# One of seven weight products: its low part from a VectorE subtraction instead of an accumulating GpSimd transfer

## The chip, the cores and the metric

The kernel runs on one core of a Trainium2 chip. The metric is device time of one launch in microseconds (us); the median of three runs is shown for the kernel before. The profiled execution is a fourth run of the same program, and all durations below come from it.

## The reference, cut to what matters

A two-layer block over 256 latent tokens (x) and 256 context tokens (c), 1024 features each. Every layer is half-step SwiGLU FFN, a mixer with three branches, and a second FFN:

```
def swiglu(u, w1, w3, w2):
    return (jax.nn.silu(u @ w1) * (u @ w3)) @ w2

def ffn_sublayer(h, mod, w1, w3, w2, g, b):
    u = h * (1 + mod[1]) + mod[0]
    return layer_norm(ALPHA * h + 0.5 * mod[2] * swiglu(u, w1, w3, w2), g, b)
```

All matrices are float32, w1 and w3 are 1024 x 2816, w2 is 2816 x 1024. Only the products with w1 and w3 of two of the four FFNs are touched by the change.

## The kernel before, in words

Each float32 operand is split into a high part (fp32r, rounded) and a low part (what is left), and a product is three matmuls: high x high, high x low, low x high. The high part is a ScalarE (ACT) copy, the low part a VectorE (DVE) subtraction; `split_into` (L228) does both. Weights stream from HBM through five `raw` buffers, loaded by SyncE's queue (SP), into five high and five low buffers (the names end in `hi` and `lo`).

In two FFNs (the second of layer 0 and the first of layer 1) the 18 hidden tiles 4 to 21 don't multiply w1 and w3 by x and c one by one. `wquads` (L193) forms sums of quarters of both weight tiles, `Blocks` sums of the operands, and seven block products of 12 matmuls each (128x128 by 128x256) replace eight. So there are 36 such tiles. Of each, `wquads` makes four weight pairs: **wa** (the w1 tile as it is), **wd** (the second half of the w3 tile), **wc** (sums written over the w1 buffer), **wb** (sums written over the w3 buffer, `r3`). The sums are the four DVE additions L214 to L217. For wa, wd and wc, `split_into` is used. For wb the low part is made in another way: ACT writes the high part (L222), ACT copies it negated into the low buffer (L223), and a DMA from GpSimd's queue adds `r3` to it in place (L224).

The order on the matmul engine (PE) is written out in `more` (L614), with `blocks_end` keeping the blocks in line. For one tile: two blocks on wa; one on wd of the tile before (`x_blocks`); one on wc (`third_block`, operand tH); one on wc of the tile before (`ctx_blocks`, operand op); two on wb (`last_blocks`, L590, operand tH). In a block, the third matmul (L265) is the first that reads a low part. After each block DVE and ACT take its result from PSUM: ACT L575 copies the first wa block into cc, L594 the last wb block into cv; DVE L583, L595, L601, L606, L608 combine 128x256 tiles; ACT L229 and DVE L230 split the finished 128x512 tile into gh and gl. Between them DVE runs jobs of the conditioning vector in the background (L289, L291, `acc`, 128x512 each, on `araw` loads through the same five raw buffers).

Instructions of one engine run in the order that the scheduler of the framework fixed when the program was built; `high_priority` lets the weight work of a tile go ahead of the tile's own products. Buffers are taken in that order too: as the trace shows, the high part of wb waits until PE has left the high part of wa of the same tile.

Of the kernel before, what the change touches and what calls it, by code (L numbers as in the profile page):

```python
# [8 lines left out]
F32 = mybir.dt.float32  # L9
F32R = mybir.dt.float32r  # L10
AF = mybir.ActivationFunctionType
ALU = mybir.AluOpType
# [39 lines left out]
def hybrid_kernel(tc, x, ctx, pos, cc, wada, pcol, w1, w3, w2a, w2b, wst, wv, wg, wbr, wout, dfc, dft, idn, lnrow, out):  # L52
    nc = tc.nc
# [11 lines left out]
    def nm(s):  # L65
        cnt[0] += 1
        return f"{s}_{cnt[0]}"
# [32 lines left out]
    act = nc.scalar.activation  # L100
# [75 lines left out]
    def tick():  # L176
        debt[0] += rate[0]
        n = int(debt[0])
        debt[0] -= n
        bg(n)  # L180
# [12 lines left out]
    def wquads(src1, src3):  # L193


        tick()
        H = slice(0, 512), slice(512, 1024)
        with tc.high_priority(offset=PRE):
            raw = []
            for src in (src1, src3):  # L200
                t = wp.tile([P, 1024], F32, tag="raw", bufs=NR, name=nm("raw"))
                nc.sync.dma_start(out=t, in_=src)
                raw.append(t)
            r1, r3 = raw

            def halves(name, w=1024):
                return [wp.tile([P, 1024], F32R, tag=t, bufs=NW, name=nm(name + t))[:, :w] for t in ("hi", "lo")]

            a = halves("wa")
            split_into(a[0], a[1], r1)  # L210
            d = halves("wd", 512)
            split_into(d[0], d[1], r3[:, H[1]])
            add = dict(op=ALU.add)
            V.tensor_tensor(r3[:, H[1]], r3[:, H[0]], r3[:, H[1]], **add)  # L214
            V.tensor_tensor(r3[:, H[0]], r3[:, H[0]], r1[:, H[0]], **add)
            V.tensor_tensor(r1[:, H[0]], r3[:, H[1]], r1[:, H[0]], **add)
            V.tensor_tensor(r1[:, H[1]], r1[:, H[0]], r1[:, H[1]], **add)  # L217
            c = halves("wc")
            split_into(c[0], c[1], r1)

            b = halves("wb")
            act(b[0], r3, AF.Copy)  # L222
            act(b[1], b[0].bitcast(F32), AF.Copy, scale=-1.0)  # L223
            nc.gpsimd.dma_start(out=b[1].bitcast(F32), in_=r3, accum_op=ALU.add)  # L224

        return (a, 0), (a, 512), (d, 0), (b, 512), (c, 0), (b, 0), (c, 512)

    def split_into(h, l, src):  # L228
        first = act(h, src, AF.Copy)  # L229
        return first, V.tensor_tensor(l, src, h.bitcast(F32), op=ALU.subtract)  # L230
# [304 lines left out]
    def ffn(l, i, X, ys, T, nxt):  # L535
# [32 lines left out]
        def start_blocks(ft):  # L568

            f = dict(ft=ft, W=wquads(w1[l, i, ft], w3[l, i, ft]))  # L570
            f["r1"] = bank(mmp, "q1")[:, XR]
            f["c"], f["v"] = aslot("cc"), aslot("cv", 256)
            Q[:] = X.operands()
            block(f["r1"], f["W"][0], Q[0], True)
            act(f["c"][:, XR], f["r1"], AF.Copy)  # L575
            return f
# [539 lines left out]
    for part in range(4):  # L1116
# [4 lines left out]
        for kt in range(0, KT, 2):  # L1121
            raw = wp.tile([P, 1024], F32, tag="raw", bufs=NR, name=nm("araw"))
            for k in range(2):
                nc.sync.dma_start(out=raw[:, 512 * k:512 * k + 512].rearrange("p (v c) -> p v c", v=2),
                                  in_=wada[0, (kt + k) * P:(kt + k + 1) * P, 0:2 * D]
# [189 lines left out]
```

## Time and profile before

| | us |
|---|---|
| median of 3 runs (lowest, highest) | 2718.05 (2713.5, 2718.81) |
| profiled execution | 2721.58 |
| its span | 2719.8 |
| PE busy | 2538.8 |
| DVE busy | 1966.5 |
| ACT busy | 1109.8 |
| GpSimd busy | 80.5 |

The span is the time from the first to the last instruction of the profiled execution; around it lie 1.8 us. Busy times of engines overlap, so they don't add up. Matmuls are pipelined: at full clock a row of 0.28 us starts about 0.11 us after the row ahead of it. PEclk in a windows view is the clock that was granted to PE, as a share of 2.4 GHz.

The block products are two parts of the program, from 1224 to 1577 us and from 1674 to 2025 us. Each has three runs of tiles (3, 8 and 7), with products of w2 between them.

### The profile page before, as it was taken

The numbers are of one execution on the slowest core, as the hardware profiler recorded it, in microseconds if no ns is written. First come the engines' busy times: TensorE is split into PE (matmuls) and PEld (weight loads), VectorE is DVE, ScalarE is ACT, GpSimd is POOL, SyncE is SP. The second block draws the span as 40 slices with busy tenths as digits, with TensorE's granted clock in tenths as the row PEclk, the third lists the DMA queues.
The fourth block names the chain that finished last, engine by engine and source line by source line (L and its number), as shares of the span: only waits on it lengthen the run. The fifth ranks groups of instructions, "written<-read, shape, count | busy, mean of one in ns | idle before, by whom it ended". The sixth has DMA issues, their size and how long they took to land. (4 is left out here: it accounts for less than half of the span.)

```text
span 2719.8 us, 40624 instructions
## 1 busy us (share of the span) xinstructions
PE 2538.8 (93%) x15842; PEld 2231.9 (82%) x15842; DVE 1966.5 (72%) x3611; ACT 1109.8 (41%) x1834; POOL 80.5 (3%) x162
## 2 busy tenths in 40 slices
PE   8999999999999999998879799878889999999998
PEld 4777779788778888897767788777779888999998
DVE  5888887888777755587666568656556988987655
ACT  4222235333332324353442446343445334455543
POOL 0000000010100000000000000000000000000000
PEclk9999999999999999998889899988899999999999
DMA  9666663222133233326454444546353333556563
GB/s 287 197 207 191 190 199 108 90 67 89 59 102 96 67 128 97 120 86 170 111 130 133 115 132 133 146 132 178 106 142 99 106 116 119 176 166 210 159 197 125
DMA packets 135744, 372.99 MB, mean 137 GB/s; under 512 B 13313, under 2 KB 28929, under 8 KB 135553
## 3 DMA queue, kind: packets, MB, share of 16 engines
q1 hardware_dynamic: 130368, 351.53, 41.4%
q0 software_dynamic: 5184, 18.88, 3.7%
q8 instruction: 124, 2.03, 0.3%
q14 instruction: 68, 0.55, 0.1%
HBM read 344.11 MB, written 7.34 MB: 129 GB/s over the span
## 5 line engine op out<-in xcount | busy, mean ns | idle before, releaser
L189 ACT ACTIVATE whi<-raw 128x1024 fp32r<-128x1024 f32 (+1 forms) x426 | 444.1, 1044 | 872.6 <-issue 170.1
L190 DVE TENSOR_TENSOR wlo<-raw,whi 128x1024 fp32r<-128x1024 f32 (+1 forms) x426 | 511.5, 1202 | 278.7 <-ACT whi L189 275.6
L673 DVE SCALAR_TENSOR_TENSOR cy<-cz,dww,cy 128x482 f32<-128x482 f32 (+29 forms) x480 | 288.9, 602 | 17.4 <-ACT cy L765 10.5
L291 DVE SCALAR_TENSOR_TENSOR acc<-araw,sc,acc 128x512 f32<-128x512 f32 x392 | 275.1, 746 | 18.2 <-DMA araw<-in_wada_dram 17.3
L265 PE MATMUL q<-tH,wblo 128*128 128x256 f32 x288 | 109.5, 380 | 113.9 <-DMA wblo<-raw 113.9
L265 PEld LDWEIGHTS q<-tH,wblo 128*128 128x128 f32 x288 | 79.0, 274 | 122.5 <-DMA wblo<-raw 122.5
L242 PE MATMUL ffps<-op,whi 128*128 128x256 f32 x608 | 165.3, 281 | 3.9 <-ACT op L229 3.9
L243 PE MATMUL ffps<-op,whi 128*128 128x256 f32 x608 | 168.1, 280 | 0.0
L244 PE MATMUL ffps<-op,wlo 128*128 128x256 f32 x608 | 167.5, 279 | 0.0
L242 PE MATMUL ffps<-opH,whi 128*128 128x512 f32 x352 | 141.0, 403 | 0.7 <-ACT opH L229 0.7
L243 PE MATMUL ffps<-opL,whi 128*128 128x512 f32 x352 | 140.7, 400 | 0.0
L244 PE MATMUL ffps<-opH,wlo 128*128 128x512 f32 x352 | 140.1, 400 | 0.4 <-DVE wlo L190 0.4
L242 PE MATMUL w2ps<-gh,whi 128*128 128x512 f32 x336 | 134.2, 399 | 0.0
L244 PE MATMUL w2ps<-gh,wlo 128*128 128x512 f32 x336 | 133.5, 397 | 0.0
L243 PE MATMUL w2ps<-gl,whi 128*128 128x512 f32 x336 | 133.1, 396 | 0.0
L242 PE MATMUL mg<-opH,whi 128*128 128x512 f32 (+1 forms) x384 | 129.7, 338 | 0.0
L244 PE MATMUL mg<-opH,wlo 128*128 128x512 f32 (+1 forms) x384 | 129.5, 337 | 0.0
L243 PE MATMUL mg<-opL,whi 128*128 128x512 f32 (+1 forms) x384 | 129.4, 337 | 0.0
L242 PEld LDWEIGHTS ffps<-op,whi 128*128 128x128 f32 x608 | 113.0, 190 | 4.8 <-ACT op L229 4.3
L243 PEld LDWEIGHTS ffps<-op,whi 128*128 128x128 f32 x608 | 115.1, 190 | 0.2
L244 PEld LDWEIGHTS ffps<-op,wlo 128*128 128x128 f32 x608 | 114.8, 189 | 0.0
L263 PE MATMUL q<-tH,wbhi 128*128 128x256 f32 x288 | 102.7, 357 | 0.0
(390 smaller groups left out, 7358.0 us busy)
## 6 DMA issues: line engine op xcount, KB each, us to landing
raw<-in_w_dram SPq DMA_DIRECT2D x176, 512.0 KB, 4.1
raw<-in_wst_dram SPq DMA_DIRECT2D x144, 512.0 KB, 3.5
araw<-in_wada_dram SPq DMA_DIRECT2D x128, 512.0 KB, 4.2
raw<-in_w2b_dram SPq DMA_DIRECT2D x64, 512.0 KB, 4.2
raw<-in_wbr_dram SPq DMA_DIRECT2D x48, 512.0 KB, 3.5
wblo<-raw POOLq DMA_DIRECT2D x36, 512.0 KB, 5.3
raw<-in_w2a_dram SPq DMA_DIRECT2D x32, 384.0 KB, 3.2
araw<-in_wada_dram SPq DMA_DIRECT2D x32, 256.0 KB, 5.7
```

Of the source, the lines that this page charges most:

```text
L189: act(hi, raw, AF.Copy)
L190: V.tensor_tensor(lo, raw, hi.bitcast(F32), op=ALU.subtract)
L242: PE.matmul(ps, wh, xh, start=first and i == 0, stop=False)
L243: PE.matmul(ps, wh, xl, start=False, stop=False)
L244: PE.matmul(ps, wl, xh, start=False, stop=last and i == n - 1)
L263: PE.matmul(ps, wh, xh, start=first and k == 0, stop=False, **how)
L265: end = PE.matmul(ps, wl, xh, start=False, stop=k == 3, **how)
L291: V.scalar_tensor_tensor(accs[s], w, c, accs[s], op0=ALU.mult, op1=ALU.add)
L673: V.scalar_tensor_tensor(dv[:, :, a:b], sv[:, :, a + o:b + o], wcols[:, j:j + 1], dv[:, :, a:b], op0=ALU.mult, op1=ALU.add)
```

## The change

The low part of wb is made as the other three are, by `split_into`: one ACT copy for the high part and one DVE subtraction (128x1024) for the low part. The negated ACT copy and the accumulating transfer go.

```
             c = halves("wc")
             split_into(c[0], c[1], r1)
-
             b = halves("wb")
-            act(b[0], r3, AF.Copy)
-            act(b[1], b[0].bitcast(F32), AF.Copy, scale=-1.0)
-            nc.gpsimd.dma_start(out=b[1].bitcast(F32), in_=r3, accum_op=ALU.add)
+            split_into(b[0], b[1], r3)
```

Lines after L223 have a number lower by 3 in the changed kernel: L230 is L227 there, L606 is L603, L595 is L592.

On DVE, in the third run of tiles of the second part, before (wclo, walo, wdlo are low parts; cc and cv are the tile's 128x256 results; the additions of the next tile's weights stand as `raw`):

```order
L217 TENSOR_TENSOR raw_16875<-raw_16875 128x512
L595 TENSOR_TENSOR cv_16769<-q_2575_16843,cv_16769 128x256
L291 SCALAR_TENSOR_TENSOR acc_16870<-araw_17135,sc,acc_16870 128x512 x2
L230 TENSOR_TENSOR wclo_16892<-raw_16875,wchi_16891 128x1024
L583 TENSOR_TENSOR cc_16901<-q_2591_16916,cc_16901 128x256
L601 SCALAR_TENSOR_TENSOR cc_16768<-q_2569_16767,cc_16768 128x256
L230 TENSOR_TENSOR walo_17012<-raw_17007,wahi_17011 128x1024
L606 TENSOR_TENSOR cc_16768<-q_2575_16843,cc_16768 128x256
L230 TENSOR_TENSOR wdlo_17016<-raw_17009,wdhi_17015 128x512
```

The same place on DVE now:

```order
L592 TENSOR_TENSOR cv_16737<-q_2575_16811,cv_16737 128x256
L217 TENSOR_TENSOR raw_16843<-raw_16843 128x512
L288 SCALAR_TENSOR_TENSOR acc_16838<-araw_17101,sc,acc_16838 128x512
L580 TENSOR_TENSOR cc_16868<-q_2591_16883,cc_16868 128x256
L288 SCALAR_TENSOR_TENSOR acc_16838<-araw_17101,sc,acc_16838 128x512
L227 TENSOR_TENSOR wclo_16860<-raw_16843,wchi_16859 128x1024
L227 TENSOR_TENSOR wblo_16864<-raw_16845,wbhi_16863 128x1024
L227 TENSOR_TENSOR walo_16979<-raw_16974,wahi_16978 128x1024
L598 SCALAR_TENSOR_TENSOR cc_16736<-q_2569_16735,cc_16736 128x256
L603 TENSOR_TENSOR cc_16736<-q_2575_16811,cc_16736 128x256
L227 TENSOR_TENSOR wdlo_16983<-raw_16976,wdhi_16982 128x512
```

The subtraction for wblo stands between those for wclo and walo, the step on cv has moved ahead of L217, and the step on cc (L583, now L580) ahead of wclo.

On ACT at the same tile, before:

```order
L594 ACTIVATE cv_16769<-q_2569_16767 128x256
L229 ACTIVATE wchi_16891<-raw_16875 128x1024
L575 ACTIVATE cc_16901<-q_2588_16900 128x256
L222 ACTIVATE wbhi_16895<-raw_16877 128x1024
L223 ACTIVATE wblo_16896<-wbhi_16895 128x1024
L229 ACTIVATE wahi_17011<-raw_17007 128x1024
```

And now:

```order
L591 ACTIVATE cv_16737<-q_2569_16735 128x256
L572 ACTIVATE cc_16868<-q_2588_16867 128x256
L226 ACTIVATE wchi_16859<-raw_16843 128x1024
L226 ACTIVATE wbhi_16863<-raw_16845 128x1024
L581 ACTIVATE cc_16868<-cc_16868 128x256
L226 ACTIVATE wahi_16978<-raw_16974 128x1024
```

The negated copy is gone, and wchi now comes after the copy of the first wa block (L575, now L572). On GpSimd the 36 transfers are gone and nothing else moved; on SP the loads keep their order; on PE the block products keep theirs within a run of tiles.

## Rows read from the trace of the kernel before

**Rows 1.** The page: busy time, share of the span and instructions of each engine.
```profile
PE 2538.8 (93%) x15842; PEld 2231.9 (82%) x15842; DVE 1966.5 (72%) x3611; ACT 1109.8 (41%) x1834; POOL 80.5 (3%) x162
```

**Rows 2.** Waits of the whole span: engine, line, releaser, us in total, times, longest.
```profile
PE q L265 <- DMA wblo<-raw: 113.9, 36, 5.8
```

**Rows 3.** The tile wblo: count, duration ns min/median/max, first and last start; landing times.
```profile
L223 ACT ACTIVATE wblo<-wbhi x36: 1042/1046/1062, 1228.0 to 2015.0; 128x1024 fp32r<-128x1024 f32 x36
DMA to landing us min/median/max: 4.5/5.3/8.3
```

**Rows 4.** Windows: each run's first L575 to its last; one of six, and sum.
```profile
core 0: us, PE busy (x) PEld busy (x) DVE busy (x) ACT busy (x) POOL busy (x), PEclk, DMA share, GB/s
...
1919.84:2012.36 92.52, 71.30 (x515) 69.73 (x514) 53.76 (x88) 42.01 (x67) 5.17 (x6) 0.85 0.48 126
sum 445.83, PE 344.00 PEld 335.83 DVE 271.63 ACT 200.80 POOL 24.28; mean PE 57.33 PEld 55.97 DVE 45.27 ACT 33.47 POOL 4.05
```

**Rows 5.** Windows: the last tile of each run, from L575 to L594; sum.
```profile
sum 88.26, PE 70.83 PEld 65.27 DVE 45.41 ACT 41.67 POOL 6.20; mean PE 11.81 PEld 10.88 DVE 7.57 ACT 6.95 POOL 1.03
```

**Rows 6.** Timeline of one wb: start, us, engine, line, operation [idle before, releaser].
```profile
1921.15 1.06 ACT L222 ACTIVATE wbhi<-raw 128x1024 fp32r<-128x1024 f32 x1 [0.92 <-PE q L264]
1922.42 1.04 ACT L223 ACTIVATE wblo<-wbhi 128x1024 fp32r<-128x1024 f32 x1
...
1923.76 0.86 POOL L224 DMA_DIRECT2D wblo<-raw  x1 [58.26 <-ACT wblo L223]
...
1925.08 0.28 PE L263 MATMUL q<-tH,wbhi 128*128 128x256 f32 x1
...
1928.79 0.58 PE L265 MATMUL q<-tH,wblo 128*128 128x256 f32 x1 [3.33 <-DMA wblo<-raw]
1929.17 0.41 PE L263 MATMUL q<-tH,wbhi 128*128 128x256 f32 x1
```

**Rows 7.** Timeline of PE: two other waits for wblo.
```profile
1266.03 0.58 PE L265 MATMUL q<-tH,wblo 128*128 128x256 f32 x1 [2.18 <-DMA wblo<-raw]
...
1762.28 0.39 PE L265 MATMUL q<-tH,wblo 128*128 128x256 f32 x1 [1.29 <-DMA wblo<-raw]
```

**Rows 8.** Windows right behind three waits: the third last column is PEclk.
```profile
1928.80:1934.80 6.00, 6.00 (x28) 6.00 (x29) 1.85 (x5) 0.91 (x2) 0.00 (x0) 0.50 0.29 87
1762.30:1765.20 2.90, 2.90 (x24) 2.90 (x25) 1.93 (x4) 0.02 (x1) 0.00 (x0) 1.00 0.58 156
1266.10:1269.30 3.20, 3.20 (x15) 3.20 (x16) 0.72 (x2) 0.00 (x0) 0.00 (x0) 0.51 0.67 209
```

**Rows 9.** Timeline of PE: first matmuls of two blocks, and first use of wclo.
```profile
1952.18 0.28 PE L263 MATMUL q<-tH,wdhi 128*128 128x256 f32 x1
...
1953.54 0.28 PE L263 MATMUL q<-tH,wchi 128*128 128x256 f32 x1
...
1953.77 0.28 PE L265 MATMUL q<-tH,wclo 128*128 128x256 f32 x1
```

**Rows 10.** Timeline of DVE and ACT in the same tile.
```profile
1950.08 0.42 DVE L595 TENSOR_TENSOR cv<-q,cv 128x256 f32<-128x256 f32 x1 [3.92 <-ACT cv L594]
1950.42 1.53 DVE L291 SCALAR_TENSOR_TENSOR acc<-araw,sc,acc 128x512 f32<-128x512 f32 x2
...
1954.39 1.04 ACT L229 ACTIVATE wahi<-raw 128x1024 fp32r<-128x1024 f32 x1
...
1955.46 1.22 DVE L230 TENSOR_TENSOR walo<-raw,wahi 128x1024 fp32r<-128x1024 f32 x1 [1.30 <-ACT wahi L229]
1956.60 0.42 DVE L606 TENSOR_TENSOR cc<-q,cc 128x256 f32<-128x256 f32 x1
...
1960.60 0.69 DVE L217 TENSOR_TENSOR raw<-raw 128x512 f32<-128x512 f32 x1
```

**Rows 11.** Lines of DVE, third run of the second part: busy, mean ns, idle before.
```profile
L230 DVE TENSOR_TENSOR walo<-raw,wahi 128x1024 fp32r<-128x1024 f32 x6 | 7.4, 1226 | 8.2 <-ACT wahi L229 8.2
```

**Rows 12.** DMA issues in the same run: KB, median us to landing.
```profile
raw<-in_w_dram SPq DMA_DIRECT2D x9, 512.0 KB, 3.6
```

## The prediction

> **What bounds the kernel now.** I read the page's busy times first, then the waits of the whole span, then the timeline around the longest of them.
>
> PE is busy for 93% of the span, DVE for 72%, ACT for 41% [rows 1]. So PE sets the time, and what it waits for is what can be won. In the list of waits one line stands out: PE waits 36 times, 113.9 us in all, at L265 for the transfer that makes wblo, 3.16 us each [rows 2]. It is once per hidden tile of the block products; ACT's negated copy ahead of it runs 36 times as well [rows 3].
>
> The timeline shows how one such wait comes about [rows 6]. The copy wbhi starts at 1921.15, when PE has left the buffer it takes. The negated copy starts at 1922.42, GpSimd issues the transfer at 1923.76. PE starts the first wb block at 1925.08; its third matmul, the first one on wblo, starts at 1928.79, 3.33 us late. From the end of wbhi (1922.21) to that matmul it is 6.6 us, most of it the transfer, which takes 4.5 to 8.3 us to land [rows 3].
>
> The wait costs a second time. The matmuls behind it have rows of 0.41 us and not 0.28 [rows 6]: in the 6 us after the 3.33 us wait the granted clock is 0.50, the lower level of 1.2 GHz [rows 8]. After a wait of 2.18 us [rows 7] it is 0.51 over the next 3.2 us; after one of 1.29 us it stays at 1.00, that is 2.4 GHz [rows 7, 8].
>
> How much that is can be seen in the six runs of tiles. From the first L575 of each run to its last there are 30 periods of one tile, 445.83 us in all, 14.86 us each; the run shown has a mean clock of 0.85 [rows 4]. A block of 12 matmuls at full clock takes 1.36 us (1953.54 less 1952.18 [rows 9]), so the 84 of a tile take 9.52 us and 30 tiles 285.6 us. PE was busy for 344.0 of the 445.8 us [rows 4]: about 102 us are waits and 58 us are the lower clock.
>
> **What the change removes.** Per tile the negated copy (1.05 us of ACT), the issue on GpSimd (0.86 us), and the transfer [rows 3, 6]. Only the transfer's 6.6 us chain lies on the path. ACT's time was cover, since it is busy for 200.8 of 445.8 us [rows 4], and I cost it at nothing; without that cover it would be worth at most 1.05 us per tile. The buffer of r3 was free again when the transfer had landed, and is free after the subtraction now, which lets SP's loads start earlier, not later.
>
> **What it adds and moves.** 36 subtractions of 128x1024 on DVE. The nearest row, walo, has the same shape and types and takes 1.226 us [rows 11], so 1.23 x 36 = 44 us of DVE. DVE's order is changed around it: wblo stands between wclo and walo, cv is ahead of L217, and in most tiles the step on cc (L583) is ahead of wclo. Behind wblo on DVE wait walo, for the next tile's first block, and the two cc steps, L601 and L606, for this one's result.
>
> First, is wblo there in time? From the start of wbhi (1921.15) to the first wb matmul (1925.08) PE had three other blocks to do, 3.93 us, and two matmuls more before it wants wblo: 4.15 us [rows 6]. The copy takes 1.06 us of that and the subtraction 1.23. So the wait at wblo goes, as long as ACT and DVE together come to it no more than 1.8 us late.
>
> What is late next? The one loop left, from tile to tile, goes through DVE. I follow it in a tile of before, counting from the first matmul on wclo (1953.77 [rows 9]). L606 starts at +2.83, after the two wc blocks; L217, the last of the weight additions of the next tile, starts at +6.83 [rows 10]. Up to there nothing is removed. Now cv comes ahead of L217 (0.42 us long, about 0.3 in the queue [rows 10]) and L217 takes 0.69. ACT's wchi follows: from the start of such a copy to the start of its subtraction it is 1.07 us (1954.39 to 1955.46), and the subtraction takes 1.22 [rows 10]. So the next tile's first matmul on wclo can start at 6.83 + 0.3 + 0.69 + 1.07 + 1.22 = 10.1 us. This is longer than PE's 9.52 us, so PE waits 0.6 us at wclo.
>
> Background work lengthens the loop. Two acc steps take 1.53 us [rows 10] between L217 and wclo; 1.07 of it lies beside wchi, and in half of the tiles the cc step (0.42) is there too: 10.5 to 10.9, I take 10.7. With four steps two lie further ahead in the loop, 0.75 each: 10.7 + 1.5 = 12.2 at most, 11.5 if the gap at L606 hides half; I take 11.8. In the changed order of DVE, 12 of the 30 periods have at most one step, 13 two or three, 5 four or more.
>
> The sum: 12 x 10.1 + 13 x 10.7 + 5 x 11.8 = 319 us in place of 445.8, a gain of 126.5. The last tile of each run (six, 88.26 us in all [rows 5]) has its wait as well; I give it 3.16 less the mean new wait of 319/30 - 9.52 = 1.1, so 6 x 2.1 = 12. The lower clock I take as gone: the new waits of 0.6 to 2.3 us are on average nearer to the 1.29 us of [rows 7] than to 2.18. For steps of the in-order queues that meet badly I take off 0.2 us per tile, 7 us; it is a choice. In all 131.5 us. The profiled execution took 2721.58 us (span 2719.8), so 2590. The median of the runs shown is 3.5 us lower, which gives **2586 us**.
>
> The gain has a floor and a ceiling. If PE waited for nothing, 445.8 - 285.6 = 160 and 6 x 3.16 = 19 would be won: 2539 by the median. Below, the rivals set the end.
>
> **The rivals.**
>
> *PE's floor.* The loop through DVE turns out shorter than PE's 9.52 us, for example because cv costs nothing ahead of L217 and the copies start earlier. For it: ACT is freed. Against it: the steps from L606 to L217 are rows of before and not touched. 2539 to 2555 us.
>
> *DVE becomes the bound.* It is busy for 271.6 of the 445.8 us [rows 4]; with 30 x 1.23 that is 308, or 10.3 us per tile, already above PE's 9.52. Before, walo waited for its high part in each tile, 8.2 us over six [rows 11], 1.37 each. If that stays, a tile takes 11.6 us; if wblo now waits as long at the head of the queue, 13.0 us. Gains: 30 x (14.86 - 11.6) + 12 = 110 and 56 + 12 = 68: 2608 to 2650 us. Against it: in my loop walo's high part is written while DVE does wblo. The Trainium skill, "Perfetto Trace Analysis", section "Optimizing Scalar/DVE Operations", advises to move work to ScalarE when DVE is saturated; by that rule this change goes the wrong way, and the trace agrees that DVE is the busier of the two.
>
> *The lower clock stays.* PE still waits once per tile, now at wclo, and if each wait draws a slow stretch, the 22 matmuls from there to the end of the second wc block take 2.5 us longer, and they lie in the loop: 13.2 us per tile, a gain of 50 and 12, 2656 us. Against it is the 1.29 us wait, behind which the clock was 1.00 [rows 7, 8]. The Trainium skill, "TensorE: Matmul & The Clock Gate", section "A second HAM failure mode: psum-queue depth-cycling", has a kernel whose short but frequent idle times between groups of matmuls kept the clock falling back. No row here shows it for waits as short as these.
>
> *Slower.* One mechanism: the loads. A faster tile asks for its two 512 KB weight tiles more often. The slot of r3 is free about 1.2 us after the first matmul on wclo, and its content two tiles on is wanted at L606's time of the next tile, 10.7 + 2.8 us later: 12 us for a landing that takes 3.6 us [rows 12]. The tile gets as long as before only when the landing takes over 12 + 4.2 = 16 us. At 17 us: 30 x 0.8 lost, 2742 us. Nothing in the profile is near it.
>
> **How the numbers follow.** My forecast, 2565 to 2610 us by itself: 0.60. PE's floor 0.09, DVE the bound 0.19, the lower clock 0.09, slower 0.03. The range of 2550 to 2645 leaves out the deeper half of the floor case, most of the clock case and the slower one. A measurement here can tell about 0.2% (5 us) from no change. All cases but the last are faster: 0.96; within 0.2%: 0.02, for a mixture of clock and loads that just eats the gain; slower: 0.02.
>
> **What would show it.** The line "PE q L265 <- DMA wblo" is gone, and a wait for wclo of about 1 us stands in its place, 30 times or more. From L575 to L575 it is 10 to 12 us. PEclk in the runs of tiles is above 0.95, DVE's busy share there above 90%, ACT's still near half. GpSimd shows no transfer. I am wrong on the path if PE's wait is still at wblo, now for DVE; wrong on the clock if PEclk stays near 0.85; wrong on the loop if the wait for wclo is over 2 us on tiles without background steps, or if ACT or SP end it.

## The result and the profile after

| | us |
|---|---|
| kernel before, median of 4 runs (lowest, highest) | 2718.43 (2713.5, 2727.44) |
| changed kernel, median of 4 runs (lowest, highest) | 2567.39 (2563.01, 2570.35) |
| ratio, 95% interval | 0.944 (0.9411 to 0.9468) |
| profiled execution of the changed kernel, its span | 2566.58, 2564.6 |

The changed kernel is faster by 151 us by the medians, and by 155.0 us by the two profiled executions. The forecast was 2586, with a range of 2550 to 2645, so the time came out 19 us lower and inside the range.

The page after: busy time, share of the span and instructions of each engine.

```profile
PE 2484.3 (97%) x15842; PEld 2182.5 (85%) x15842; DVE 1999.5 (78%) x3647; ACT 1076.8 (42%) x1798; POOL 49.1 (2%) x126
```

Against [rows 1], DVE has 36 instructions and 33.0 us more, ACT 36 and 33.0 us less, GpSimd 36 fewer. PE runs the same 15842 matmuls in 54.5 us less busy time. No work was taken from PE; more of it ran at the higher clock. In the profiled executions the mean granted clock went from 0.967 to 0.991.

The waits of the changed kernel: engine, line, releaser, us in total, times, longest. L262 is the line that was L265.

```profile
ACT wchi L226 <- DVE raw L217: 29.2, 28, 4.0
...
PEld q L262 <- DVE wclo L227: 19.9, 27, 1.3
...
PE q L262 <- DVE wclo L227: 14.1, 24, 1.1
```

The 113.9 us of [rows 2] have no line any more. In its place PE waits for wclo, 24 times, 0.59 us each, and the line of ACT above it shows what stands behind that wait: wchi waits for DVE's last weight addition.

The tile wblo, which answers to [rows 3]: its instruction, and what DVE waited for ahead of it.

```profile
L227 DVE TENSOR_TENSOR wblo<-raw,wbhi x36: 1216/1219/1226, 1227.9 to 1863.8; 128x1024 fp32r<-128x1024 f32 x36
its engine sat idle before it (us, times) until:
  ACT wbhi L226: 1.1, 2
```

Subtraction by subtraction, DVE pays 1.22 us, and it nearly never stands still for wbhi: 1.1 us over all 36 tiles.

Windows of the changed kernel from the first L572 of each run of tiles to its last (columns as in [rows 4]); one run of six, and the sum. Behind it the same view for the last tile of each run, which answers to [rows 5].

```profile
1798.26:1860.52 62.26, 59.23 (x515) 58.04 (x514) 57.95 (x92) 35.41 (x60) 0.97 (x2) 1.00 0.42 136
sum 308.28, PE 295.33 PEld 288.83 DVE 285.67 ACT 170.37 POOL 0.97; mean PE 49.22 PEld 48.14 DVE 47.61 ACT 28.39 POOL 0.16
```

```profile
sum 65.76, PE 60.34 PEld 56.66 DVE 54.84 ACT 40.05 POOL 0.08; mean PE 10.06 PEld 9.44 DVE 9.14 ACT 6.67 POOL 0.01
```

The 30 periods of a tile take 308.28 us, 10.28 each, in place of 14.86. The granted clock is 1.00 in five of the six runs and 0.89 in the first. DVE is busy for 93% of these stretches, ACT for 55%. The shares show how near DVE now is to being full, and yet PE is busy for 96%.

The 155.0 us are thus: 137.6 in the 30 periods (445.83 less 308.28), 22.5 in the six last tiles (88.26 less 65.76), and 5 us given back in the rest of the program. Of the 137.6, PE's idle time is 88.9 us (101.8 before [rows 4], 12.95 now). The other 48.7 us are the same matmuls at a higher clock: the windows count 2527 of them before and now, busy for 344.00 us and 295.33 us.

### The profile page after: what moved, and what is told of

Read it like the earlier page. It is cut to its first block, busy times and chain, and to the rows that moved or that the text cites. A ratio compares the mean times of both kernels' runs of the same rounds, so it can differ in the third digit from the quotient of the medians.

```text
span 2564.6 us, 40463 instructions
## 1 busy us (share of the span) xinstructions
PE 2484.3 (97%) x15842; PEld 2182.5 (85%) x15842; DVE 1999.5 (78%) x3647; ACT 1076.8 (42%) x1798; POOL 49.1 (2%) x126
## 5 line engine op out<-in xcount | busy, mean ns | idle before, releaser
L239 PE MATMUL qk<-opH,whi 128*128 128x512 f32 (+1 forms) x296 | 103.2, 349 | 0.0
L240 PE MATMUL qk<-opL,whi 128*128 128x512 f32 (+1 forms) x296 | 102.1, 345 | 0.0
L241 PE MATMUL qk<-opH,wlo 128*128 128x512 f32 (+1 forms) x296 | 101.8, 345 | 0.0
```

The costliest lines, as they stand in the source:

```text
L239: PE.matmul(ps, wh, xh, start=first and i == 0, stop=False)
L240: PE.matmul(ps, wh, xl, start=False, stop=False)
L241: PE.matmul(ps, wl, xh, start=False, stop=last and i == n - 1)
```

## The experiments

Two theories stood against each other for each part. On the gain: that it comes from a shorter chain to wblo (the copy and the transfer), or from the clock that PE's waits cost. On what is left: that the loop from L606 (now L603) over L217, wchi and wclo sets the tile, or that DVE's busy time does.

**Filling the wait, chain untouched.** The kernel before, with 24 matmuls whose result is thrown away ahead of the first wb block.

```
+            (hi, lo), c = f["W"][3]
+            with tc.issue_after(blocks_end[-1].ins):
+                for k in range(24):
+                    end = PE.matmul(f["r3"], hi[:, c:c + P], Q[3][0][0], start=True, stop=True)
+            blocks_end[:] = [end]
```

> The kernel before, with 24 matmuls of no use (128x128 by 128x256, high part of wb by tH, into the bank that the next block overwrites) ahead of the first wb block of each of the 36 tiles. They take 24 x 0.113 = 2.7 us at full clock and fill most of the 3.16 us in which PE waits for wblo. Nothing of the chain to wblo is shortened. Theory (the wait costs a second time, through the clock): PEclk in the runs of tiles rises from 0.85 to above 0.95, the wait line shrinks from 113.9 us to 10 to 30 us, and the time falls by 45 to 65 us, to 2655 to 2675 us. Rival (the lower clock is a companion and the pace is set by the chain from wa's end to wblo alone, which includes the slow matmuls only by chance): 2712 to 2730 us, with the same waits elsewhere.

Measured: 2672.82 us, 0.9817 of the kernel before (0.9789 to 0.9844), 45 us less. Its windows of the runs of tiles, one and the sum, and its line of waits:

```profile
1873.52:1953.25 79.73, 76.47 (x659) 75.10 (x658) 53.10 (x87) 41.89 (x67) 5.17 (x6) 1.00 0.55 146
sum 398.93, PE 379.60 PEld 372.16 DVE 271.82 ACT 201.40 POOL 24.28; mean PE 63.27 PEld 62.03 DVE 45.30 ACT 33.57 POOL 4.05
```

```profile
PE q L265 <- DMA wblo<-raw: 22.7, 24, 2.7
```

The transfer lands in 4.8 us (median; 5.3 before), and PE has more to do, but the clock in the run shown goes from 0.85 to 1.00 and the 30 periods from 445.83 to 398.93 us. Does the transfer's half microsecond explain a part of that? No: the filler in the periods (30 x 2.7 = 81 us) and PE's idle time (19.3) come to 100 us, about the 101.8 that stood idle before. So nearly all of the 46.9 us is the clock: idle time was replaced by useless work, and the useful work ran faster. The wait's second price was real. So about 45 of the 151 us were to be had without shortening the chain; the other 106 came only with the shorter one. The windows are those of the profiled execution, 2663.35 us, 9 us below the median, so they show rather more than the 45 us.

**The transfer's traffic alone.** The changed kernel, which also sends r3 to an unused buffer in HBM from GpSimd's queue.

```
             split_into(b[0], b[1], r3)
+            nc.gpsimd.dma_start(out=junk, in_=r3)
```

> The changed kernel, with 36 transfers of 512 KB back again on GpSimd's queue: r3 is copied to a scratch in HBM that nobody reads, after the subtraction's input is complete. r3's buffer is free only when it has landed, as before the change. Theory (only the wait for the landing was on the path): the same as the changed kernel within 6 us, 2562 to 2574 us. Rival (a part of the gain came from the transfer's share of the DMA engines, or from r3's buffer being free earlier): 15 to 60 us slower than the changed kernel, with waits of ACT for raw loads.

Measured: 2569.87 us, ratio 0.9444 (0.942 to 0.9468), no different from the changed kernel. The 18.88 MB are back in the queue, at no price that can be seen. They are a lighter load than the accumulating transfers, 1.9% of the 16 DMA engines' time where those took 3.7%. So what cost time was waiting for the transfer; that it ran beside the loads cost nothing at half of its load, and at the full load it wasn't tested. Nor did this run hold r3 for longer, though it was meant to. Here is one tile, on GpSimd and on DVE, and the landing times:

```profile
1838.56 0.53 POOL L223 DMA_DIRECT2D junk<-raw  x1 [10.18 <-DVE raw L216]
```

```profile
1842.91 1.22 DVE L229 TENSOR_TENSOR wblo<-raw,wbhi 128x1024 fp32r<-128x1024 f32 x1
```

```profile
DMA to landing us min/median/max: 2.9/2.9/4.1
```

The transfer has landed before DVE's subtraction, which reads r3 too, begins, here as in each of the 36 tiles. What it was worth that r3 is free earlier than in the kernel before stays untested; there the block products' copies of loaded weights, wahi and wdhi, waited for a load only 4 times, 3.8 us in all.

**One step more in the loop.** The changed kernel with a DVE instruction behind L217 that leaves its 128x512 tile as it is.

```
             V.tensor_tensor(r1[:, H[1]], r1[:, H[0]], r1[:, H[1]], **add)
+            V.tensor_tensor(r1[:, H[1]], r1[:, H[1]], r1[:, H[1]], op=ALU.max)
```

> The changed kernel, with one more DVE operation of 128x512 per tile (maximum of the sum with itself, so nothing changes) behind L217, the last of the weight additions. Theory (the loop from tile to tile goes through DVE from L603 by L217 to wclo): 0.6 to 0.7 us per tile in 30 of the 36 tiles, 15 to 25 us slower than the changed kernel, 2582 to 2592 us, and PE's waits for wclo grow by that. Rival (PE is the bound now, DVE has slack): within 5 us of the changed kernel.

Measured: 2595.83 us, ratio 0.9533 (0.9509 to 0.9557), 28 us above the changed kernel; 36 x 0.69 is 25. The expected range ended at 2592, so it was missed by 4 us. Its waits:

```profile
PE q L263 <- DVE wclo L228: 20.0, 28, 1.1
...
PE q L261 <- ACT wchi L227: 13.3, 23, 1.3
```

PE now waits 23 times for the high part of wc as well, together 33.3 us, where the changed kernel has 17.5 for the two. PE's busy time on the page rose too, from 2484.3 to 2495.5 us with as many matmuls: the granted clock was below 1.00 in five of the six runs, and in one of the changed kernel's. The expectation had left that out. All of the step comes through to the end, as it must if it lies in the loop. It would come through by DVE's busy sum too; the next run tells these two apart.

**wc in two halves.** The changed kernel, with the first 512 columns of wc split ahead of L217, which writes only the other 512. DVE's instructions grow in number and its work doesn't shrink; only the order and the pieces change.

```
-            V.tensor_tensor(r1[:, H[1]], r1[:, H[0]], r1[:, H[1]], **add)
             c = halves("wc")
-            split_into(c[0], c[1], r1)
+            split_into(c[0][:, H[0]], c[1][:, H[0]], r1[:, H[0]])
+            V.tensor_tensor(r1[:, H[1]], r1[:, H[0]], r1[:, H[1]], **add)
+            split_into(c[0][:, H[1]], c[1][:, H[1]], r1[:, H[1]])
```

> The changed kernel, with wc made in two halves of 128x512: the half that the third block reads needs only L216, the other L217. The loop from L603 to the first matmul on wclo gets about 1 us shorter (0.63 in place of 1.05 on ACT, 0.68 in place of 1.22 on DVE), DVE gets 0.14 us more per tile. Theory (the loop's latency is the bound): the waits for wclo go, 0.5 us in 25 tiles, and the time falls by 8 to 14 us, to 2553 to 2560 us. Rival (DVE's sum of work is the bound, 9.5 us of 10.3 per tile being busy): no change, 2564 to 2572 us, with the wait at another low part.

Measured: 2546.23 us, ratio 0.9355 (0.9331 to 0.938), 21 us below the changed kernel and below what either theory gave (2553 to 2560, and 2564 to 2572). Windows of its runs of tiles, two and the sum, and the tile wclo:

```profile
1421.87:1480.58 58.71, 58.71 (x529) 58.39 (x528) 56.30 (x100) 37.07 (x67) 0.00 (x0) 1.00 0.36 118
...
1652.81:1724.73 71.92, 71.92 (x620) 71.25 (x618) 68.59 (x117) 43.89 (x79) 0.00 (x0) 1.00 0.44 140
...
sum 298.46, PE 294.35 PEld 290.96 DVE 286.54 ACT 176.24 POOL 1.06; mean PE 49.06 PEld 48.49 DVE 47.76 ACT 29.37 POOL 0.18
```

```profile
L228 DVE TENSOR_TENSOR wclo<-raw,wchi x72: 675/685/694, 1223.3 to 1839.8; 128x512 fp32r<-128x512 f32 x72
its engine sat idle before it (us, times) until:
  DVE wclo L228: 1.6, 3
```

In the two runs shown PE is never idle. The wait for wclo that was 14.1 us is gone but for one of 0.6 us. DVE is busy as long as in the changed kernel (286.5 us and 285.7), but in 298.5 us and not 308.3, so its sum did not bound the changed kernel: the loop did. The profiled executions lie 17.6 us apart (this one is 2.7 us above its median): 9.8 in the periods, 10.6 in the last tiles of the runs (65.8 to 55.2 us), and about 3 given back in the rest. The split between periods and last tiles isn't sharp, since the copy that bounds these stretches comes later among PE's matmuls here (2563 of them in the periods, 2527 in the changed kernel). The expectation had counted the waits for wclo alone, 12.5 us; PE's idle time in periods and last tiles together fell by 14.3. The Trainium skill, "Perfetto Trace Analysis", section "Optimizing Scalar/DVE Operations", says that engines that aren't full but cause bubbles on others may gain from instructions broken up; here it holds with DVE 93% busy. This version beats both kernels.

**Was ACT's copy cover?** The changed kernel, with a second ACT copy of wbhi onto itself between the first one and the subtraction.

```
-            split_into(b[0], b[1], r3)
+            act(b[0], r3, AF.Copy)
+            act(b[0], b[0].bitcast(F32), AF.Copy)
+            V.tensor_tensor(b[1], r3, b[0].bitcast(F32), op=ALU.subtract)
```

> The changed kernel, with one more ACT copy of 128x1024 per tile between the high part of wb and the subtraction (the high part is copied onto itself), where the negated copy stood before. So the copy is back on the way to wblo, the transfer is not. Theory (the transfer was what cost, the copy lay under other work): wblo is written about 1 us later, within its 1.8 us of slack, so within 10 us of the changed kernel, 2565 to 2578 us, and no wait of PE for wblo of 1 us or more. Rival (the copy was a part of the wait): 36 x 1.05 = 38 us slower, 2605 us.

Measured: 2573.88 us, ratio 0.9445 (0.9418 to 0.9472), no different from the changed kernel. Waits of DVE and PE:

```profile
DVE wblo L223 <- ACT wbhi L222: 19.9, 26, 1.3
PE q L264 <- DVE wclo L229: 16.2, 26, 0.9
```

DVE now stands still for 19.9 us ahead of wblo, and PE's wait for wclo is what it was, 16.2 us. DVE's wait at wblo comes behind wclo; that what it delays, walo and the cc steps, had room for it is inferred from the time, not shown. So once the transfer is gone, the copy costs nothing that the intervals can tell (about 7 us to either side). What it would have brought to take the copy alone out of the old chain, where it was 1.05 of the 6.6 us, wasn't tested.

**The subtraction on GpSimd.** The changed kernel, with wblo by a GpSimd instruction in place of DVE's.

```
-            split_into(b[0], b[1], r3)
+            act(b[0], r3, AF.Copy)
+            nc.gpsimd.tensor_tensor(b[1], r3, b[0].bitcast(F32), op=ALU.subtract)
```

> The changed kernel, with the subtraction for wblo done by GpSimd's own arithmetic (tensor_tensor, 128x1024) and not by DVE. DVE is rid of 1.2 us per tile. No run so far shows how long GpSimd takes for it. Theory (any engine will do that has it ready within the 4.15 us less 1.06 us of the copy, about 3 us): if GpSimd takes under 3 us, the loop through DVE gets shorter where DVE was full, 2550 to 2567 us. If it takes longer, PE waits at wblo again for the excess: at 4 us 36 us more than the changed kernel, at 6 us 110 us more and the lower clock again. Rival (with the transfer gone the place of the subtraction doesn't matter): 2560 to 2575 us whatever GpSimd takes.

Measured: 2572.95 us, ratio 0.9456 (0.9421 to 0.9491), no different from the changed kernel. The theory had given 2550 to 2567 for a duration under 3 us, and missed: the duration was under 3 us, the gain didn't come. The time is in the rival's range (2560 to 2575), but not for the rival's reason, that the place doesn't matter. GpSimd's and DVE's timelines around one walo, and walo over all 36 tiles:

```profile
1848.04 2.66 POOL L222 TENSOR_TENSOR wblo<-raw,wbhi 128x1024 fp32r<-128x1024 f32 x1 [8.00 <-ACT wbhi L221]
```

```profile
1847.23 1.22 DVE L228 TENSOR_TENSOR wclo<-raw,wchi 128x1024 fp32r<-128x1024 f32 x1
1848.36 0.42 DVE L581 TENSOR_TENSOR cc<-q,cc 128x256 f32<-128x256 f32 x1
1848.70 0.41 DVE L599 SCALAR_TENSOR_TENSOR cc<-q,cc 128x256 f32<-128x256 f32 x1
1849.03 2.75 DVE L228 TENSOR_TENSOR walo<-raw,wahi 128x1024 fp32r<-128x1024 f32 x1
```

```profile
L228 DVE TENSOR_TENSOR walo<-raw,wahi x36: 1209/2362/2823, 1217.2 to 1859.9; 128x1024 fp32r<-128x1024 f32 x36
```

walo lasts 2.75 us here in place of 1.22, and 2.36 by the median. It ends at 1851.78, 1.08 us after GpSimd has ended (1850.70), which is about its own length. In 27 of the 36 tiles walo starts while GpSimd is at wblo, and in each it ends 1.1 us after it; in the other nine it takes 1.2 us. The two steps on cc, which read one operand from PSUM, run beside GpSimd at 0.41 us as ever. What DVE is spared at wblo it loses at walo: over the 30 periods it is busy for 287.8 us, and for 285.7 in the changed kernel. The Trainium skill, "SBUF — State Buffer", section "Who interferes with whom", has that a DVE instruction with both inputs in SBUF contends with a GpSimd instruction that reads SBUF, and that the later one waits until the first is done; the trace agrees.

## Why the prediction was right, and where it was off

**What bounds the kernel.** That the transfer's chain held PE once per tile, and that the wait cost a second time through the clock, are both shown: the wait is gone with the transfer, and filling the wait alone gave 45 us. "58 us are the lower clock" was somewhat high: it was 48.7 us, as told above. The forecast took PE's work as the 84 block matmuls of a tile, 9.52 us, but PE is busy for 9.84 us of each period even now, so that base was too low; what the difference consists of wasn't taken apart.

**What the change removes.** ACT's copy at nothing, and the transfer's traffic at nothing: both agree with their runs, within the limits named there.

**What it adds.** 1.23 us was forecast for the subtraction, 1.22 measured. That wblo would be there in time is right: no wait of PE names it.

**The loop.** The timeline of the changed kernel in a tile of the sixth run, on PE, ACT and DVE: the first matmul on wclo of two tiles that follow on each other, and the steps between.

```profile
1832.79 0.39 PE L262 MATMUL q<-tH,wclo 128*128 128x256 f32 x1 [0.92 <-DVE wclo L227]
...
1843.28 0.39 PE L262 MATMUL q<-tH,wclo 128*128 128x256 f32 x1 [0.69 <-DVE wclo L227]
```

```profile
1840.74 1.06 ACT L226 ACTIVATE wchi<-raw 128x1024 fp32r<-128x1024 f32 x1 [0.67 <-DVE raw L217]
```

```profile
1835.60 0.42 DVE L603 TENSOR_TENSOR cc<-q,cc 128x256 f32<-128x256 f32 x1 [0.27 <-PE q L262]
...
1839.63 0.42 DVE L592 TENSOR_TENSOR cv<-q,cv 128x256 f32<-128x256 f32 x1
1839.96 0.68 DVE L217 TENSOR_TENSOR raw<-raw 128x512 f32<-128x512 f32 x1
1840.56 1.53 DVE L288 SCALAR_TENSOR_TENSOR acc<-araw,sc,acc 128x512 f32<-128x512 f32 x2
1842.01 1.22 DVE L227 TENSOR_TENSOR wclo<-raw,wchi 128x1024 fp32r<-128x1024 f32 x1
1843.15 1.22 DVE L227 TENSOR_TENSOR wblo<-raw,wbhi 128x1024 fp32r<-128x1024 f32 x1
1844.28 1.22 DVE L227 TENSOR_TENSOR walo<-raw,wahi 128x1024 fp32r<-128x1024 f32 x1
```

From the first matmul on wclo, L603 starts at +2.81 (forecast 2.83) and L217 at +7.17 (6.83 + 0.3 = 7.13). The two acc steps run beside wchi and past its end, and the next tile's matmul on wclo starts at +10.49 (10.5 to 10.9 for two acc steps). The chain is the predicted one, step by step, and DVE goes from wclo to wblo to walo without a stop.

**The signs.** The wait for wblo is gone, DVE is busy for 93% of the periods and ACT for 55%, and GpSimd has no transfer: as forecast. Two signs were off. PE's wait for wclo was forecast at about 1 us, 30 times or more, and came 24 times at 0.59 us; since PE has 9.84 us to do in a period and not 9.52, less of the loop is left to wait. And PEclk was above 0.95 in five of the six runs, but 0.89 in the first.

**The size.** The working gave 131.5 us, the profiled executions show 155.0. Three terms were mis-sized:

- *The 30 periods*: 126.5 less an allowance of 7 for queues that meet badly, and 137.6 measured. The allowance wasn't needed. The other 11 us are mostly in four periods, those of the first run of each part, which the forecast had counted as 2 x 11.8, 10.7 and 10.1 = 44.4 by their background steps (10, 0, 2 and 4 between one wblo and the next). They took 7.99, 9.89, 8.17 and 8.83 us, 34.9 in all. The very first tile of a part has no wd block and no second wc block of a tile before it, so at most 60 block matmuls and not 84, and the loop isn't closed yet. The other 26 periods took 273.4 us, and the forecast for them was 319.3 - 44.4 = 274.9. That is nearer than its parts deserve: 11 periods with at most one background step took 10.46 us on average (forecast 10.1), 12 with two or three 10.44 (10.7), three with four or more 11.01 (11.8). The misses cancel, so the close sum is in part luck; by these averages a background step costs less than was forecast.
- *The last tiles of the runs*: 12 us forecast, 22.5 measured. PE's idle time in them fell from 17.4 us to 5.4, so the 12 us for the wait were right. PE's busy time fell as well, from 70.83 [rows 5] to 60.34 us, and that was left out. The clock rose (0.88 to 1.00 in the tile shown below), and there are fewer matmuls: 508 in the six last tiles before, 484 now. Those that are gone are of the products that follow, whose rows start 0.23 us apart, so 24 of them are about 5.5 of the 10.5 us (an estimate from these rows); the other 5 are the clock.
- *The rest of the program*: nothing forecast, 5 us lost. The five stretches between the runs of tiles grew from 259.95 to 263.94 us, with 1537 matmuls in place of 1518. These are matmuls that PE did in the wait of a run's last tile before, and does behind it now. So most of the 5 us is not a new cost: it was counted as a gain of the last tiles.

The last tile of the first run before, and the same one now (columns as in [rows 4]):

```profile
1256.75:1271.03 14.28, 12.10 (x96) 11.16 (x95) 7.71 (x15) 6.40 (x12) 0.87 (x1) 0.88 0.65 181
```

```profile
1250.74:1260.25 9.51, 9.51 (x89) 8.85 (x88) 7.15 (x12) 6.28 (x10) 0.00 (x0) 1.00 0.48 146
```

The two terms that were too small outweigh the third. The remaining 4 us are in where the profiled executions lie beside their medians: 3.5 us above before, 0.8 below after.

**The rivals.** DVE as the bound, which had 0.19: at 93% busy it came near, but walo waited for nothing that the trace shows, and the version with wc in halves went below it with the same DVE work. The lower clock: not there in five of the six runs, with waits of 0.59 us on average. PE's floor, 2539 to 2555 us: not reached by the change, which leaves the 14.1 us for wclo, but by the version with wc in halves. The loads: the loads of a 512 KB tile in the sixth run land in 3.6 us as before [rows 12], and no wait of PE in the block products names one; ACT's copies wahi and wdhi wait for one 5 times, 6.5 us in all.

## What to carry to other kernels

Follow the longest repeated wait of the bounding engine back to what makes it, and price that chain, not the busy shares: here work went from an engine that was 41% busy to one that was 72% busy, and the time fell by 5.6%. Then find the next loop in the trace of before and go round it instruction by instruction; away from the ends of the runs it gave the sum of the new periods within 1% and each kind of period within 7%, and showed which step to shorten next. Price the first and the last round of a loop by themselves, with the clock, since that is where the forecast was off.

## What the runs showed that was not expected

- Doing nothing was dearer than doing useless work: 24 matmuls per tile without a use (24 rows 0.11 us apart, 2.7 us per tile) brought 45 us, since the granted clock stayed at 1.00, the 2.4 GHz level, where it had been 0.85 in the run shown.
- Waits of 0.59 us in most tiles, 1.1 at the longest, left the granted clock at 1.00 in five of six runs. In the first it was 0.89, and there PE had just stood idle for 7.04 us, with rows of 0.42 us behind it:

```profile
1233.28 0.58 PE L260 MATMUL q<-tH,wchi 128*128 128x256 f32 x1 [7.04 <-ACT cc L572]
1233.66 0.42 PE L261 MATMUL q<-tL,wchi 128*128 128x256 f32 x1
```

- With a step more in the loop, and waits for wchi and wclo that follow each other, it was 0.94 over the second run:

```profile
1296.00:1380.00 84.00, 75.97 (x605) 73.47 (x604) 75.89 (x122) 41.62 (x70) 0.00 (x0) 0.94 0.36 116
```

- A GpSimd subtraction of 128x1024 takes 2.49 us (median of 36), twice DVE's 1.22, and a DVE subtraction that starts beside it and reads both inputs from SBUF ended 1.1 us after it, in all 27 tiles where the two met.
